# Gate products one step behind their one-hots, and the last group's v tiles loaded with its up tiles

## The chip, the cores and the metric

The kernel runs on one core of one Trainium2 chip, as one program. The metric is the device time of one execution in microseconds. Before the change three timed executions took 3132.31, 3131.12 and 3117.97 us, median 3131.12 us; a fourth execution was profiled.

## The reference, cut to what matters

The reference is one layer of an encoder over 1024 tokens of width 1024, in float32. A mixing part (a convolution module and an RWKV-7 recurrence beside each other) ends in an output projection and a layer norm. The second part is a retrieval over 128 x 128 = 16384 experts of one neuron each. The change touches the second part only:

```
q = (h2 @ peer_wq).reshape(bsz, seq, 8, 256)
s1 = einsum('bshd,hnd->bshn', q[..., :128], peer_k1)
s2 = einsum('bshd,hnd->bshn', q[..., 128:], peer_k2)
...                                   # top 16 of each, top 16 of the 256 sums
experts = i1 * 128 + i2 ;  gates = softmax(top scores)
z = einsum('td,tkd->tk', h, peer_u[experts])
y2 = einsum('tk,tkd->td', gelu(z) * gates, peer_v[experts])
x = layer_norm(ALPHA * x + gate2 * y2, ln2_g, ln2_b)
```

## The kernel before

**Two ways to the retrieval.** The 1024 tokens are eight tiles of 128. For three of them (tiles 5 to 7) the kernel gathers the rows of the chosen experts with indirect DMAs that POOL issues (L1273), and DVE sums them up (L1279, L1286). For the other five (the dense tiles, 640 tokens) it computes all 16384 experts with matmuls, and multiplies each expert's activation by a gate that is zero for experts that the token did not choose. That takes a matrix of gates with one entry for each token and expert, which has to be built first.

**The gate matrix.** `gate_matrix` is a generator, one for each dense tile, that the rest of the program steps. For each token the matrix is the product of two one-hot matrices: the first index of each of the token's 128 choices, and the second index times the gate. Eight tokens at a time, DVE compares the indices with a row of numbers (two `mask` tiles, L1094). Four tokens at a time, a quad, the masks become float32 operands: `oa` by ACT (L1100), `ob` by POOL for three tokens (L1101) and by ACT for the fourth (L1103). Then four matmuls `mgate<-oa,ob` (L1108), and ACT copies the result into a `stage` tile (L1109); after eight quads the stage is written to memory (G_d, L1116). A tile has 32 quads, so the five tiles have 160 quads and 640 product matmuls. Buffers: two for `oa`, three for `ob`, three for the masks, three PSUM banks for `mgate`, two stages.

**What steps it.** In the first stretch of the program (conv, RWKV, up to about 1000 us) `fill` calls `step(gates)` each 12th time. Then follows a loop, `while side or slow or gates`, in which the out-projection of the last tokens (L870, its norm on DVE from L874), the query projection (L216), the keys (L942, copied out by ACT at L945) and the choice of the top 16 are the side work. Each 12th turn it calls `step(gates)` inside `tc.high_priority(offset=GPRI)`, so that everything a step emits is put forward. The order of the instructions on each engine is then fixed by a scheduler with priorities, which has its own model of times; each engine runs its instructions in that order, and waits where an operand is not there. SP issues the plain DMAs, ACT those of the stages, POOL the gathers.

**The dense loop.** 32 groups follow, each of four e's (128 experts apiece). An e's up matmuls (L1418, 48 of them into two PSUM banks) are followed by a gelu on ACT (L1420), the multiplication by the gates on DVE (L1422), and a split into a high part `ah` (ACT, L1423) and a low part `al` (DVE, L1424); the down matmuls (L1434) take three products of high and low parts. The weights are split as they come: a load into a `raw` buffer (L1310, three buffers for u and v tiles), the high part by ACT (L1314), the low part by POOL (L1316: `ulo`, `vlo`). A group's v tiles are loaded two e's later than its u tiles. For group 31 each v tile is multiplied by a row of gate2 first (DVE, L1312).

**The end.** `finish` runs the down products of group 31, and ends the five dense tiles. It loads the last two v tiles, loads the five residual tiles `xres` into buffers that become free (two with the tag raw, two in uhi, one in ulo), finishes the gathers, multiplies the sums by gate2 (L1358), adds them to the residuals (L1363 on DVE, L1361 on POOL), and then for each tile and half adds the down product (L1372, for the last tile L1375), takes the norm, and multiplies and adds its two rows (ACT L1391, DVE L1392 and L1393), before the store (L1394).

## Time and profile before

| | us |
|---|---|
| median of the three timed executions | 3131.12 |
| profiled execution | 3123.78 |
| its span in the trace | 3122.0 |
| granted TensorE clock, mean | 0.968 |
| first stages, up to | 1000 |
| out-projection, queries and gate work | 1000 to 1285 |
| gate quads behind the last query matmul | 1285 to 1322.7 |
| dense loop and gathers | 1322.7 to 3102.3 |
| behind PE's last matmul | 3102.3 to 3122 |

PE is TensorE, DVE VectorE, ACT ScalarE, POOL GpSimd, and SP the engine that issues plain DMAs. A row of a stretch gives the busy time of each engine in it. A row of a group of instructions gives the line, the engine, the operation, the tiles as out<-in and the count, then the busy time and the mean of one in ns, and behind the second bar the idle time of the engine just before them and what ended it. The chain of waits is followed back from the last instruction, and its rows give a start, a length and what ran. A matmul in float32 leaves two records here, so "x8" of gate products in the chain is one quad.

### The profile page before, as it was taken

The numbers are of one execution on the slowest core, as the hardware profiler recorded it, in microseconds if no ns is written. First come the engines' busy times: TensorE is split into PE (matmuls) and PEld (weight loads), VectorE is DVE, ScalarE is ACT, GpSimd is POOL, SyncE is SP. The second block draws the span as 40 slices with busy tenths as digits, with TensorE's granted clock in tenths as the row PEclk, the third lists the DMA queues.
The fourth block names the chain that finished last, engine by engine and source line by source line (L and its number), as shares of the span: only waits on it lengthen the run. The fifth ranks groups of instructions, "written<-read, shape, count | busy, mean of one in ns | idle before, by whom it ended". The sixth has DMA issues, their size and how long they took to land.

```text
span 3122.0 us, 54848 instructions
## 1 busy us (share of the span) xinstructions
PE 2942.9 (94%) x20416; PEld 2604.9 (83%) x20416; DVE 2393.5 (77%) x5392; ACT 1186.8 (38%) x2238; POOL 1810.1 (58%) x1419
## 2 busy tenths in 40 slices
PE   6979999988899889999999999999999999999997
PEld 4748667877778788898998899989899898999986
DVE  6276764446877989369999999987888787777878
ACT  5562452333346667842322323322223232222324
POOL 2434112224253443487776786877778677787874
PEclk9989999969889999999999999999999999999998
DMA  8868766768666887899999998999999989999995
GB/s 312 312 207 301 265 183 205 268 221 299 216 217 241 314 332 278 327 350 336 328 330 327 316 344 314 352 352 330 339 344 338 356 322 340 341 338 349 328 352 196
DMA packets 431852, 945.77 MB, mean 303 GB/s; under 512 B 92465, under 2 KB 234209, under 8 KB 411105
## 3 DMA queue, kind: packets, MB, share of 16 engines
q1 hardware_dynamic: 318112, 497.62, 47.2%
q0 software_dynamic: 110592, 402.70, 34.5%
q10 hardware_dynamic: 2880, 41.94, 3.3%
q8 instruction: 160, 2.62, 0.3%
q14 instruction: 108, 0.88, 0.1%
HBM read 800.76 MB, written 141.39 MB: 302 GB/s over the span
## 4 chain that ended last, share of the span: by engine, by line
PE 64%; DVE 20%; DMA 7%; ACT 4%; issue 3%; POOL 1%; SPq 0%; ACTq 0%; DVEq 0%; POOLq 0%
PE mg L1418 23%; PE md L1434 22%; PE mm L216 7%; PE mm L870 2%; DMA cw<-cond_w 2%; DVE grow L1279 2%; PE mm L528 2%; DVE mask L1094 1%; PE mgate L1108 1%; DVE gy L1286 1%; DVE cw L303 1%; PE bank L707 1%; DMA grow<-peer_v,eid 1%; PE bank L733 1%; DVE oh L1023 1%
## 5 line engine op out<-in xcount | busy, mean ns | idle before, releaser
L1418 PE MATMUL mg<-h2h,uhi 128*128 128x320 f32 x2024 | 626.6, 310 | 7.3 <-DVE al L1424 6.5
L1418 PE MATMUL mg<-h2h,ulo 128*128 128x320 f32 x2024 | 625.9, 309 | 0.0
L1418 PE MATMUL mg<-h2l,uhi 128*128 128x320 f32 x2024 | 625.6, 309 | 0.0
L1434 PE MATMUL md<-vhi,al 128*128 128x512 f32 x1260 | 490.6, 390 | 0.0
L1434 PE MATMUL md<-vlo,ah 128*128 128x512 f32 x1260 | 489.1, 390 | 0.0
L1434 PE MATMUL md<-vhi,ah 128*128 128x512 f32 x1260 | 485.1, 390 | 1.9 <-DVE yacc L1452 1.9
L1286 DVE SCALAR_TENSOR_TENSOR gy<-grow,gz,gy 128x1024 f32<-128x1024 f32 x349 | 446.1, 1278 | 10.7 <-DMA grow<-peer_v,eid 9.6
L1279 DVE SCALAR_TENSOR_TENSOR grow<-grow,gh 128x1024 f32<-128x1024 f32 x365 | 438.1, 1210 | 16.2 <-DMA grow<-peer_u,eid 12.7
L1273 POOL DMA_INDIRECT grow<-peer_u,eid x365 | 344.5, 944 | 176.3 <-DVE grow L1279 58.0
L1273 POOL DMA_INDIRECT grow<-peer_v,eid x352 | 333.2, 947 | 164.9 <-DVE gy L1286 62.1
L1418 PEld LDWEIGHTS mg<-h2h,uhi 128*128 128x128 f32 x2024 | 380.4, 188 | 15.0 <-DVE al L1424 8.4
L1418 PEld LDWEIGHTS mg<-h2l,uhi 128*128 128x128 f32 x2024 | 380.5, 188 | 5.8
L1418 PEld LDWEIGHTS mg<-h2h,ulo 128*128 128x128 f32 x2024 | 380.4, 188 | 2.9
L1316 POOL TENSOR_TENSOR vlo<-vraw,vhi 128x1024 fp32r<-128x1024 f32 x128 | 309.1, 2416 | 26.2 <-ACT vhi L1314 22.5
L1316 POOL TENSOR_TENSOR ulo<-uraw,uhi 128x1024 fp32r<-128x1024 f32 x128 | 309.3, 2417 | 21.6 <-ACT uhi L1314 19.1
L1452 DVE TENSOR_TENSOR yacc<-md,yacc 128x512 f32<-128x512 f32 x300 | 204.6, 685 | 130.9 <-PE md L1434 97.7
L1434 PEld LDWEIGHTS md<-vlo,ah 128*128 128x128 f32 x1260 | 236.5, 188 | 47.5
L1434 PEld LDWEIGHTS md<-vhi,ah 128*128 128x128 f32 x1260 | 236.1, 188 | 47.3 <-DVE yacc L1452 2.8
L1434 PEld LDWEIGHTS md<-vhi,al 128*128 128x128 f32 x1260 | 236.5, 188 | 44.2
L1101 POOL TENSOR_TENSOR ob<-mask,selt 128x384 f32<-128x384 bf16 x160 | 140.4, 891 | 228.8 <-DVE mask L1094 99.3
L1314 ACT ACTIVATE vhi<-vraw 128x1024 fp32r<-128x1024 f32 x128 | 134.9, 1054 | 348.0 <-DMA vraw<-peer_vt 296.1
L204 POOL TENSOR_TENSOR wsplit<-wraw,wsplit 128x1024 fp32r<-128x1024 f32 x46 | 112.5, 2448 | 215.1 <-ACT wsplit L203 204.8
(430 smaller groups left out, 5868.6 us busy)
## 6 DMA issues: line engine op xcount, KB each, us to landing
uraw<-peer_ut SPq DMA_DIRECT2D x128, 512.0 KB
vraw<-peer_vt SPq DMA_DIRECT2D x128, 512.0 KB
wsplit<-split_wq SPq DMA_DIRECT2D x48, 1024.0 KB
G_d<-stage ACTq DMA_DIRECT2D x20, 2048.0 KB
gmat<-G_d SPq DMA_DIRECT2D x32, 1024.0 KB
cw<-cond_w SPq DMA_DIRECT2D x48, 512.0 KB
wsplit<-split_w_out SPq DMA_DIRECT2D x24, 1024.0 KB
split_w_in<-wsplit SPq DMA_DIRECT2D x22, 1024.0 KB
```

The lines of the kernel that those rows point to most:

```text
L204: G.tensor_sub(lo, raw, hi.bitcast(F32))
L216: T.matmul(pt, l[:, k, :], r[k], start=i == 0, stop=i == 3 * KD - 1)
L528: T.matmul(pt[:, 128 * g:128 * g + 128], dg[:, 128 * j:128 * j + 128], ubuf[ct][:, g, LAGS - 1 - m:LAGS - 1 - m + 128], start=m == 0, stop ...
L1101: G.tensor_mul(ob[:, :3], mb[:, :3], gt[:, c:c + 3, None].to_broadcast([128, 3, 128]))
L1273: G.indirect_dma_start(out=r, out_offset=None, in_=peer_u if k < 128 else peer_v, in_offset=bass.IndirectOffsetOnAxis(ap=eid[:, k % 128:k ...
L1279: V.scalar_tensor_tensor(r, r, 1.0, ht, op0=OP.mult, op1=OP.mult, accum_out=z[:, i:i + 1])
L1286: V.scalar_tensor_tensor(y, r, z[:, i - 128:i - 127], y, op0=OP.mult, op1=OP.add)
L1314: A.activation(hi, raw, AF.Copy)
L1316: G.tensor_sub(lo, raw, hi.bitcast(F32))
L1418: T.matmul(p, l[:, k, :], r[k][:, bs], start=i == 0, stop=i == 3 * KD - 1)
L1434: T.matmul(p, l[:, ts], r[:, e % 2, :], start=e == 0 and q == 0, stop=e == 3 and q == 2)
L1452: ins = V.tensor_add(ya, p, ya)
```

## The change

Three edits. **First**, the body of `gate_matrix` is cut in two: `operands` makes the masks and the one-hots of a quad, `products` its matmuls, the eviction and the store. The generator yields after each, and the products of a quad come after the operands of the next one. Both callers step twice now; in the second loop only the first of the two steps, which emits operands, stands inside `high_priority`. **Second**, each v tile of group 31 is loaded in its own e, beside the u tile, and no more in `finish`. **Third**, the residual tiles take three raw and two uhi buffers, and the small sums `fsum` move to a pool with four buffers.

```
--- before.py
+++ after.py
@@ -643,6 +643,7 @@
             slow_step(1)
         if gb and fills[0] % GSTEP == 0:
             step(gates)
+            step(gates)
 
     def pairs(n, fn):
 
@@ -1079,41 +1080,61 @@
         gt = st[:, 2]
         key = [gv[:, w].bitcast(BF).rearrange("p (t two) -> p t two", two=2) for w in range(2)]
         sh = [128, 8, 64, 2]
-        for r0 in range(0, 128, TB):
-            blocks[0] += 1
-            if st3 and tt != DT[-1] and blocks[0] % 3 == 0:
-                stage = st3[0].tile([128, 128, TB], F32, name="stage3")
+        masks = []
+
+        def operands(c):
+
+            if c % 8 == 0:
+                masks[:] = []
+                for w in range(2):
+                    m = gb[0].tile([128, 8, 128], BF, name="mask", bufs=MB)
+                    V.tensor_tensor(m.rearrange("p t (e two) -> p t e two", two=2),
+                                    iota_b.rearrange("p (e two) -> p e two", two=2)[:, None].to_broadcast(sh),
+                                    key[w][:, c:c + 8, None, :].to_broadcast(sh), op=OP.is_equal)
+                    masks.append(m)
+            ma, mb = (m[:, c % 8:c % 8 + 4] for m in masks)
+            oa, ob = quad_("oa", GB[0]), quad_("ob", GB[1])
+            A.activation(oa, ma, AF.Copy)
+            G.tensor_mul(ob[:, :3], mb[:, :3], gt[:, c:c + 3, None].to_broadcast([128, 3, 128]))
+            if c // 4 % 4 in COLA:
+                A.activation(ob[:, 3], mb[:, 3], AF.Copy, scale=gt[:, c + 3:c + 4])
             else:
-                stage = gb[0].tile([128, 128, TB], F32, name="stage", bufs=2)
-            for q in range(0, TB, 4):
-                c = r0 + q
-                if q % 8 == 0:
-                    masks = []
-                    for w in range(2):
-                        m = gb[0].tile([128, 8, 128], BF, name="mask", bufs=MB)
-                        V.tensor_tensor(m.rearrange("p t (e two) -> p t e two", two=2),
-                                        iota_b.rearrange("p (e two) -> p e two", two=2)[:, None].to_broadcast(sh),
-                                        key[w][:, c:c + 8, None, :].to_broadcast(sh), op=OP.is_equal)
-                        masks.append(m)
-                ma, mb = (m[:, q % 8:q % 8 + 4] for m in masks)
-                oa, ob = quad_("oa", GB[0]), quad_("ob", GB[1])
-                A.activation(oa, ma, AF.Copy)
-                G.tensor_mul(ob[:, :3], mb[:, :3], gt[:, c:c + 3, None].to_broadcast([128, 3, 128]))
-                if c // 4 % 4 in COLA:
-                    A.activation(ob[:, 3], mb[:, 3], AF.Copy, scale=gt[:, c + 3:c + 4])
+                V.tensor_mul(ob[:, 3], mb[:, 3], gv[:, 2, c + 3:c + 4].to_broadcast([128, 128]))
+            return oa, ob
+
+        stage = [None]
+
+        def products(c, oa, ob):
+
+            q = c % TB
+            if q == 0:
+                blocks[0] += 1
+                if st3 and tt != DT[-1] and blocks[0] % 3 == 0:
+                    stage[0] = st3[0].tile([128, 128, TB], F32, name="stage3")
                 else:
-                    V.tensor_mul(ob[:, 3], mb[:, 3], gv[:, 2, c + 3:c + 4].to_broadcast([128, 128]))
-                pt = mgate().rearrange("p (t e) -> p t e", t=4)
-                for t in range(4):
-                    T.matmul(pt[:, t, :], ob[:, t, :], oa[:, t, :], start=True, stop=True)
-                A.activation(stage[:, :, q:q + 4], pt.rearrange("p t e -> p e t"), AF.Copy)
-                yield
-            b = 4 * DT.index(tt) + r0 // TB
+                    stage[0] = gb[0].tile([128, 128, TB], F32, name="stage", bufs=2)
+            pt = mgate().rearrange("p (t e) -> p t e", t=4)
+            for t in range(4):
+                T.matmul(pt[:, t, :], ob[:, t, :], oa[:, t, :], start=True, stop=True)
+            A.activation(stage[0][:, :, q:q + 4], pt.rearrange("p t e -> p e t"), AF.Copy)
+            if q < TB - 4:
+                return
+            b = 4 * DT.index(tt) + c // TB
             part = max(i for i in range(3) if GPART[i][0] <= b)
             if part == 2:
 
-                A.activation(gfirst, stage[:, 0:4, :], AF.Copy)
-            A.dma_start(G_d[part][b - GPART[part][0]].rearrange("p g x -> p (g x)"), stage.rearrange("p e t -> p (e t)"))
+                A.activation(gfirst, stage[0][:, 0:4, :], AF.Copy)
+            A.dma_start(G_d[part][b - GPART[part][0]].rearrange("p g x -> p (g x)"), stage[0].rearrange("p e t -> p (e t)"))
+
+        made = operands(0)
+        yield
+        yield
+        for c in range(0, 128, 4):
+            now = operands(c + 4) if c < 124 else None
+            yield
+            products(c, *made)
+            made = now
+            yield
 
 
     first = inproj(1, psum, pgp)
@@ -1186,6 +1207,7 @@
         if fills[0] % TGATE == 0 or not side:
             with tc.high_priority(offset=GPRI) if GPRI else nullcontext():
                 step(gates)
+            step(gates)
 
     pg2x.close()
     dp = ctx.enter_context(tc.tile_pool(name="dp", bufs=1, side="right"))
@@ -1345,11 +1367,10 @@
         return t
 
     def finish(down, vs):
-        vs += [load_v(31, 2), load_v(31, 3)]
         xts = []
         for t in range(NT):
-            xts.append(de.tile([128, D], F32, tag="raw" if t < 2 else "uhi" if t < 4 else "ulo", name="xres",
-                               bufs=3 if t < 2 else 2))
+            xts.append(de.tile([128, D], F32, tag="raw" if t < 3 else "uhi", name="xres",
+                               bufs=3 if t < 3 else 2))
             ld(xts[t], x1_d[DT[t]])
         row_pair([(1, ln_rows[3])])
         gather_to(1)
@@ -1364,7 +1385,7 @@
         for t in range(NT):
             xt = xts[t]
             st = small.tile([128, 2, 6], F32, name="bnst")
-            sums = small.tile([128, 4], F32, name="fsum")
+            sums = gp.tile([128, 4], F32, name="fsum", bufs=4)
             for half, hs in enumerate(halves):
                 p = md() if half else mg()
                 down(t, half, p)
@@ -1406,8 +1427,8 @@
             uh, ul = u_next
             if 4 * g + e < 127:
                 u_next = load_u(4 * g + e + 1)
-            if e > 1:
-                vs.append(load_v(g, e - 2))
+            if e > 1 or g == 31:
+                vs.append(load_v(g, e if g == 31 else e - 2))
 
             ah, al = (dl.tile([128, ND], F32R, name=n_, bufs=ABUF) for n_ in ("ah", "al"))
             for bs in NBLK:
```

What each engine executes is the same in number. Up to about 1000 us, and from the last gate quad to the last group, the order is the same on every engine as well. (Lines after 646 have moved: L1108 is now L1118, L942 is L943, L1418 is L1439, L1273 L1295, L1316 L1338, L1358 L1379, L1361 L1382, L1375 and L1376 L1396 and L1397, L1392 and L1393 L1413 and L1414.)

On PE, about the last key matmuls of the query, with the first up matmul of the dense loop behind them, before:

```order
L1108 MATMUL mgate<-oa,ob 128x128 x4
L216 MATMUL mm<-h2hi,wsplit 128x256
L216 MATMUL mm<-h2lo,wsplit 128x256
L216 MATMUL mm<-h2hi,wsplit 128x256
L942 MATMUL mm<-keys,qt 128x128
L1108 MATMUL mgate<-oa,ob 128x128 x4
L942 MATMUL mm<-keys,qt 128x128 x5
L1108 MATMUL mgate<-oa,ob 128x128 x4
L942 MATMUL mm<-keys,qt 128x128 x2
L1108 MATMUL mgate<-oa,ob 128x128 x8
L1418 MATMUL md<-h2h_14171,uhi 128x320
```

and now:

```order
L1118 MATMUL mgate<-oa,ob 128x128 x4
L216 MATMUL mm<-h2lo,wsplit 128x256
L216 MATMUL mm<-h2hi,wsplit 128x256
L943 MATMUL mm<-keys,qt 128x128 x6
L1118 MATMUL mgate<-oa,ob 128x128 x8
L943 MATMUL mm<-keys,qt 128x128 x2
L1118 MATMUL mgate<-oa,ob 128x128 x8
L1439 MATMUL md<-h2h_14171,uhi 128x320
```

The keys end with fewer products ahead of them: 104 of the 640 product matmuls stood behind the last key matmul, and 136 do now. In both kernels 48 up matmuls stand among these, and the last 84 and 85 products follow without any. Farther ahead, at the last twelve matmuls of the out-projection, 16 products stood directly ahead and 12 behind; now 8 ahead and 27 behind.

On POOL, near the end, from the sums of two tiles with gate2 to the last low parts of group 31 (gland is the buffer of the very last gather), before:

```order
L1358 TENSOR_TENSOR yacc<-yacc,gmat 128x1024
L1273 DMA grow<-peer_v,eid 128x1024
L1358 TENSOR_TENSOR yacc<-yacc,gmat 128x1024
L1316 TENSOR_TENSOR vlo<-vraw,vhi 128x1024
L1273 DMA grow<-peer_v,eid 128x1024 x2
L1316 TENSOR_TENSOR ulo<-uraw,uhi 128x1024
L1273 DMA grow<-peer_v,eid 128x1024 x3
L1273 DMA gland<-peer_v,eid 128x1024
L1316 TENSOR_TENSOR ulo<-uraw,uhi 128x1024
L1316 TENSOR_TENSOR vlo<-vraw,vhi 128x1024 x2
L1361 TENSOR_TENSOR xres<-xres,yacc 128x1024
```

and now:

```order
L1379 TENSOR_TENSOR yacc<-yacc,gmat 128x1024
L1338 TENSOR_TENSOR vlo<-vraw,vhi 128x1024
L1295 DMA grow<-peer_v,eid 128x1024
L1379 TENSOR_TENSOR yacc<-yacc,gmat 128x1024
L1338 TENSOR_TENSOR vlo<-vraw,vhi 128x1024
L1295 DMA grow<-peer_v,eid 128x1024
L1338 TENSOR_TENSOR ulo<-uraw,uhi 128x1024
L1295 DMA grow<-peer_v,eid 128x1024 x4
L1338 TENSOR_TENSOR ulo<-uraw,uhi 128x1024
L1295 DMA gland<-peer_v,eid 128x1024
L1338 TENSOR_TENSOR vlo<-vraw,vhi 128x1024 x2
L1382 TENSOR_TENSOR xres<-xres,yacc 128x1024 x2
```

Between the first sum and the last gather stood one vlo and one ulo; now two vlo and two ulo stand there, and the two residual adds follow each other.

On DVE, at the end, from the last tile's second add (xres<-md) on, before:

```order
L1375 TENSOR_TENSOR xres<-md,xres 128x512
L1384 TENSOR_SCALAR bnmv<-fsum 128x1
L1376 BN_STATS bnst<-xres 128x6
L1392 TENSOR_TENSOR xres<-xres,gmat 128x512
L230 BN_AGGR bnmv<-bnst 128x2
L1392 TENSOR_TENSOR xres<-xres,gmat 128x512
L1393 TENSOR_TENSOR xres<-xres,gmat 128x512
L1392 TENSOR_TENSOR xres<-xres,gmat 128x512
L1393 TENSOR_TENSOR xres<-xres,gmat 128x512
L1392 TENSOR_TENSOR xres<-xres,gmat 128x512 x2
L1393 TENSOR_TENSOR xres<-xres,gmat 128x512
L1392 TENSOR_TENSOR xres<-xres,gmat 128x512
```

and now, up to the same add, which is the last row:

```order
L1413 TENSOR_TENSOR xres<-xres,gmat 128x512
L1414 TENSOR_TENSOR xres<-xres,gmat 128x512
L1413 TENSOR_TENSOR xres<-xres,gmat 128x512
L238 RECIPROCAL rstd<-rstd 128x1
L240 TENSOR_SCALAR bnmv<-bnmv 128x1
L1396 TENSOR_TENSOR xres<-mg,xres 128x512
L1414 TENSOR_TENSOR xres<-xres,gmat 128x512
L1405 TENSOR_SCALAR bnmv<-fsum 128x1
L1414 TENSOR_TENSOR xres<-xres,gmat 128x512
L239 TENSOR_TENSOR rnew<-rstd 128x1
L1397 BN_STATS bnst<-xres 128x6
L1396 TENSOR_TENSOR xres<-md,xres 128x512
```

Before, all 20 multiplications and additions with the norm's rows stood behind that add. Now eight stand ahead of it, five of them in these rows, and twelve behind. The multiplications of the v tiles (before L1312) stood behind one another over the last group's rows; the first two now stand among the sums ahead of them.

## The prediction

> **What bounds the kernel now.** I read the page's share of busy time first, then the same by stage, then the groups of instructions of the stages that the change touches, then single rows there.
>
> ```profile
> PE 2942.9 (94%) x20416; PEld 2604.9 (83%) x20416; DVE 2393.5 (77%) x5392; ACT 1186.8 (38%) x2238; POOL 1810.1 (58%) x1419
> ```
> ```profile
> 1000.00:1120.00 120.00, 94.15 (x657) 84.16 (x653) 105.39 (x425) 77.91 (x176) 47.55 (x49) 0.96 0.84 307
> 1120.00:1285.00 165.00, 153.91 (x1291) 149.70 (x1289) 135.26 (x522) 122.59 (x282) 72.86 (x78) 1.00 0.83 314
> 1285.00:1322.70 37.70, 33.82 (x246) 30.80 (x247) 13.71 (x21) 35.15 (x78) 20.13 (x23) 1.00 0.74 263
> 1322.70:3102.30 1779.60, 1770.39 (x9932) 1614.23 (x9930) 1507.63 (x2655) 514.96 (x855) 1353.01 (x1028) 1.00 0.93 334
> 3102.30:3122.00 19.70, 0.00 (x0) 0.00 (x0) 15.51 (x45) 8.87 (x16) 0.00 (x0) 0.55 0.36 133
> ```
>
> The columns of the second fence are the stretch, its length, the busy time of PE, weight loads, DVE, ACT and POOL, then the granted clock, the DMA share and GB/s. PE bounds the whole, and most of it is the dense loop, 1322.70 to 3102.30, where PE is busy 1770.39 of 1779.60 us. The program order there is the same before and after, so that stretch gets nothing. What is left for the change is small: the two stretches in which gate work runs beside the out-projection and the queries (1000 to 1285), the gate tail behind the last query matmul (1285 to 1322.7), where ACT is busy 35.15 of 37.70 us and so sets the pace, and the end behind PE's last matmul, where only DVE and ACT work.
>
> ```profile
> L1108 PE MATMUL mgate<-oa,ob 128*128 128x128 f32 x880 | 117.2, 280 | 24.9 <-POOL ob L1101 13.2 <-ACT oa L1100 9.7 <-ACT stage L1109 1.7
> L1094 DVE TENSOR_TENSOR mask<-iota_b,selbank 128x1024 bf16<-128x1024 bf16 x107 | 71.3, 673 | 30.2 <-ACT oa L1100 13.1 <-ACT ob L1103 9.0 <-ACT selt L1074 5.8
> ```
>
> Both rows are for 1000 to 1285. PE stood 24.9 us in front of gate products: 13.2 for POOL's half of the one-hots, 9.7 for ACT's, 1.7 for an eviction. This is all that a later product can save. The masks themselves stood 30.2 us, nearly all behind ACT.
>
> **Gate stretch, step 1: products leave the query.** By the order, 104 product matmuls (26 quads of four tokens) stood behind the last key matmul of the query; now 136 (34 quads) do. So 8 quads go from the query, where PE paces, to the tail, where ACT paces.
>
> ```profile
> 1242.84 0.89 PE mgate L1108 x8
> ```
>
> A row of the chain counts two records to a matmul, so x8 is one quad: 0.89 us. The query ends 8 x 0.89 = **7.1 us earlier**.
>
> **Step 2: the tail gets longer.** Its steady pace is read from two evictions four quads apart, and what one quad costs ACT there from the groups:
>
> ```profile
> 1303.56 0.61 ACT L1109 ACTIVATE stage<-mgate 128x512 f32<-128x512 f32 x1
> ...
> 1308.71 0.64 ACT L1109 ACTIVATE stage<-mgate 128x512 f32<-128x512 f32 x1
> ```
> ```profile
> L1109 ACT ACTIVATE stage<-mgate 128x512 f32<-128x512 f32 x26 | 16.0, 626 | 0.3 <-PE mgate L1108 0.3
> L1100 ACT ACTIVATE oa<-mask 128x512 f32<-128x512 bf16 x24 | 15.8, 660 | 2.2 <-PE mgate L1108 2.2
> L1103 ACT ACTIVATE ob<-mask,selt 128x128 f32<-128x128 bf16 x23 | 8.7, 434 | 0.0
> ```
>
> (1308.71 - 1303.56) / 4 = 1.29 us for a quad, and ACT hardly waits. The order puts 34 evictions and 32 of each ACT one-hot behind ACT's last key copy, before 26, 24 and 23. Eight more quads cost 8 x 1.29 = **10.3 us**. The 48 dense matmuls that the order lets into this tail are 48 in both kernels, so they cover no more of it than before.
>
> **Step 3: waits of PE in the query.** A product stands one step behind its one-hots, so the short ACT operation directly ahead of it should be done: I take the waits on ACT as recovered, 9.7 + 1.7 = **11.4 us**. I leave the 13.2 on POOL's half, since POOL follows the masks, DVE is busy (105.39 + 135.26) of 285 us there, 84%, and the same masks and selections remain. Bounds: 0, if the waits only move, and 24.9, if all go. The front (out-projection, last tiles) is inside this term: its last 12 matmuls have x8 products directly ahead instead of x16, and x27 directly behind.
>
> The gate stretch gives -7.1 + 10.3 - 11.4 = -8.2 us, from -21.7 to +3.2 by the bounds. What SP and DVE get is covered: DVE has 36 mask operations between the last front tile and the last transpose before, 27 now, the others stand ahead; the last four h2t loads move behind score writes on SP, but seven quads of the tail still stand ahead of their first use.
>
> One rule bears on step 3.
>
> ```profile
> 1090.00:1100.00 10.00, 7.80 (x62) 7.38 (x60) 10.00 (x43) 5.25 (x13) 4.41 (x5) 1.00 0.98 399
> 1100.00:1110.00 10.00, 9.69 (x55) 9.00 (x56) 1.86 (x10) 2.41 (x5) 1.03 (x2) 0.83 0.94 358
> ...
> 1100.31 0.95 PE L1108 MATMUL mgate<-oa,ob 128*128 128x128 f32 x4 [2.50 <-POOL ob L1101]
> ```
>
> Behind a wait of 2.50 us the granted clock was 0.83 for ten us; a wait of this kind that goes would save up to 10 x 0.17 = 1.7 us beside itself. The Trainium skill, "TensorE: Matmul & The Clock Gate", Part 1 (The HAM clock gate), says that the clock is halved only after an idle window of about 3.4 us; by that rule a wait of 2.50 us costs no clock and the term is 0. The trace shows a loss all the same, and I leave the 1.7 out of the sum because this wait is one on POOL, which I keep.
>
> **The dense loop: 0.** Its rows stand in the same order on every engine.
>
> **The end, step 4: DVE's queue behind the last matmul.**
>
> ```profile
> 3101.90 0.39 PE L1434 MATMUL md<-vlo,ah 128*128 128x512 f32 x1
> ```
> ```profile
> 3116.74 0.69 DVE L1392 TENSOR_TENSOR xres<-xres,gmat 128x512 f32<-128x512 f32 x1
> 3117.35 1.29 DVE L1393 TENSOR_TENSOR xres<-xres,gmat 128x512 f32<-128x512 f32 x2
> ```
> ```profile
> L1392 DVE TENSOR_TENSOR xres<-xres,gmat 128x512 f32<-128x512 f32 x10 | 6.7, 683 | 0.8 <-ACT xres L1391 0.8
> L1393 DVE TENSOR_TENSOR xres<-xres,gmat 128x512 f32<-128x512 f32 x10 | 6.6, 684 | 0.0
> ```
>
> All 20 half-row operations of the last norm ran behind PE's last matmul. In the changed order tiles 0 and 1 are complete earlier, and 8 of the 20 stand ahead of the last tile's add. They start 0.60 us apart (3116.74 to 3117.35), so 8 x 0.60 = **4.8 us** go from the end. The first two tiles' adds come earlier too, but PE's 120 last matmuls are the same, so that alone moves nothing.
>
> **Step 5: POOL's queue ahead of the last gather.** This is the price of having the v tiles early.
>
> ```profile
> 3058.06 2.42 POOL L1316 TENSOR_TENSOR ulo<-uraw,uhi 128x1024 fp32r<-128x1024 f32 x1
> ...
> 3064.37 0.94 POOL L1273 DMA_INDIRECT gland<-peer_v,eid  x1 [0.31 <-issue]
> 3065.33 2.43 POOL L1316 TENSOR_TENSOR ulo<-uraw,uhi 128x1024 fp32r<-128x1024 f32 x1
> 3067.70 4.77 POOL L1316 TENSOR_TENSOR vlo<-vraw,vhi 128x1024 fp32r<-128x1024 f32 x2
> ```
> ```profile
> 3064.37 11.24 DMA gland<-peer_v,eid
> ...
> 3078.44 0.16 DVE al L1424
> ```
>
> The last gather (gland) was issued at 3064.37 and landed 11.24 us later; DVE waited for it, and the last al, which PE's last down products need as soon as the up matmuls end, stands behind it in DVE's queue. In the changed order one more vlo and the last ulo stand ahead of this gather: 2 x 2.42 = 4.84 us of POOL, which had no gap over 0.31 us there. So gland lands near 3080.4, al is ready 4.8 us later, and PE waits for it: **+4.8 us**. Bounds: 0, if POOL's queue has room or the gather lands faster, and about +6, if the add of a first tile (1.21 us, below) that now stands ahead of the gather's sum comes on top. The end is then -4.8 + 4.8 = 0, from -4.8 to +1.2.
>
> ```profile
> 3078.84 1.21 DVE L1363 SCALAR_TENSOR_TENSOR xres<-xres,yacc 128x1024 f32<-128x1024 f32 x1
> ...
> 3083.73 3.31 DVE L1363 SCALAR_TENSOR_TENSOR xres<-xres,yacc 128x1024 f32<-128x1024 f32 x1
> ```
> ```profile
> 3083.55 2.41 POOL L1316 TENSOR_TENSOR vlo<-vraw,vhi 128x1024 fp32r<-128x1024 f32 x1 [0.48 <-ACT vhi L1314]
> ```
>
> The same add took 1.21 us alone and 3.31 us beside a vlo of 2.41 us. The Trainium skill, "SBUF — State Buffer" (Who interferes with whom), says that a DVE operation with two SBUF inputs and a GpSimd operation that reads SBUF exclude each other through a shared port pair; the trace agrees here, with 2.1 us. This speaks against the change: POOL's two xres adds now stand together, amid DVE's adds of this form. By the rule up to two more meetings would cost 4.2 us of DVE; by the rows PE goes on with its down products until 3101.90, 18 us behind the slow add, so it is hidden, and the sum gets 0.
>
> **Sum.** -7.1 + 10.3 - 11.4 - 4.8 + 4.8 = -8.2 us. The profiled execution took 3123.78 us (span 3122.0), so its like would take 3115.6. It stands between the timed runs (3117.97, 3131.12, 3132.31); the middle two of all four have a mean of 3127.45, and 3127.45 - 8.2 = 3119.
>
> **Rivals.** (1) The step of distance covers all waits, POOL's too: 13.2 us more, -21.4, so 3127.45 - 21.4 = 3106. For it: masks are put forward alone, and they had waited 22.1 us behind ACT's one-hots, which no longer stand behind evictions put forward with them. Against: DVE at 84% and only three mask buffers. (2) The change doesn't do what it says: the scheduler had already put products where they were ready, the waits only move to other quads, and the query's gain is given back in the tail: -7.1 + 10.3 = +3.2, so 3131. For it: PE waits for gate products only 24.9 of 285 us. (3) Slower: the one-hots and not ACT's copies pace the tail. A stretch where eight quads took long is
>
> ```profile
> 1240.02 1.16 PE mgate L1108 x8
> ...
> 1256.46 0.91 PE mgate L1108 x8
> ```
>
> (the first and the last of eight quads in the chain: (1256.46 - 1240.02) / 7 = 2.35 us a quad). If masks and POOL's half can deliver a quad only each 2.35 us, also when no query work is left, 34 quads take 79.9 us where 26 took 26 x 1.29 = 33.5: +46.4, and no wait is recovered: -7.1 + 46.4 = +39.3, so 3167. It decides as soon as the one-hots come slower than ACT's 1.29 us. Against: the tail's DVE was busy 13.71 and POOL 20.13 of 37.70 us.
>
> **How the numbers follow.** Forecast 0.50 (3112 to 3126), rival 1 0.20, rival 2 0.22, rival 3 0.08. Range 3104 to 3136: it takes in most of rival 1 (less the end's gain on top) and rival 2 with the end's upper bound, and leaves out rival 3. About 0.5% (15.7 us) is what a measurement of this kernel can tell from no change: faster is under 3115.5, which is rival 1 and a quarter of the forecast, 0.33; slower is over 3146.8, rival 3, 0.08; the rest is 0.59.
>
> **What would show it.** Step 1: the last key matmul ends 7 us (with step 3, 18) earlier. Step 2: the first dense stretch begins 10 us later behind it, evictions 1.29 us apart. Step 3: idle time before the gate products near 13 us, on POOL alone. Step 4: 12 half-row operations behind PE's last matmul, and 11 us from it to the end instead of 16. Step 5: gland issued near 3069 on the old scale and a gap of 4 to 5 us of PE before its last ten down groups. It is wrong if the order's quads in the tail run apart from ACT's pace, if PE has no gap at the end, or if the dense loop changes its length.

## The result: 19 us slower, and the profile after

| | before | after |
|---|---|---|
| median of 15 timed runs, us | 3122.64 (3116.38 to 3133.92) | 3141.93 (3126.26 to 3158.54) |
| profiled execution, us | 3123.78 | 3143.16 |
| its span, us | 3122.0 | 3141.4 |

The ratio is 1.0056 with a 95% interval of 1.0045 to 1.0066: the change makes the kernel slower by 0.56%; the two medians lie 19.3 us (0.62%) apart. Forecast were 3119 and a range of 3104 to 3136.

First the line of busy time on the page of after, to be set beside the one of before:

```profile
PE 2959.7 (94%) x20416; PEld 2618.8 (83%) x20416; DVE 2381.6 (76%) x5392; ACT 1188.7 (38%) x2238; POOL 1810.7 (58%) x1419
```

The work is the same in number, and the mean granted clock is 0.961, where it was 0.968. The windows of after show where, cut at its own landmarks (columns as in the prediction: the stretch, its length, busy PE, weight loads, DVE, ACT, POOL, then granted clock, DMA share, GB/s):

```profile
1000.00:1120.50 120.50, 95.42 (x653) 86.66 (x653) 98.12 (x406) 74.32 (x169) 46.26 (x48) 0.89 0.80 292
1120.50:1280.50 160.00, 149.44 (x1232) 144.86 (x1232) 129.85 (x530) 113.53 (x257) 65.68 (x69) 0.99 0.79 296
1280.50:1337.50 57.00, 45.77 (x324) 41.48 (x322) 21.59 (x32) 48.40 (x107) 28.32 (x33) 0.94 0.77 285
1337.50:3121.60 1784.10, 1773.41 (x9939) 1613.95 (x9937) 1503.80 (x2653) 517.04 (x856) 1352.97 (x1028) 1.00 0.93 333
3121.60:3141.40 19.80, 0.00 (x0) 0.00 (x0) 16.10 (x46) 7.67 (x15) 0.00 (x0) 0.62 0.36 132
```

The third row is the gate tail: 57 us, with the clock at 0.94, where before had 1.00. ACT, which was to set its pace, is busy 85% of it, where it was 93% in the tail of before: something else holds it up.

For a comparison by stage each trace was cut at the start of the last matmul of each kind: out-projection (L870, now L871), keys (L942, L943), gate products (L1108, L1118), up (L1418, L1439) and down (L1434, L1455). The front runs from the first gate product to the last matmul of the out-projection, the query from there to the last key matmul, the tail to the last gate product, the end from the last down matmul to the end of the span. "Before again" is a second profile of the unchanged kernel.

| us | front | query | tail | dense | down | end |
|---|---|---|---|---|---|---|
| before | 213.8 | 170.6 | 39.1 | 1753.9 | 26.2 | 20.1 |
| before again | 221.1 | 171.6 | 39.1 | 1753.2 | 26.7 | 20.5 |
| after | 226.1 | 160.0 | 57.0 | 1757.8 | 25.9 | 20.2 |
| after minus before | +12.3 | -10.6 | +17.9 | +3.9 | -0.3 | +0.1 |

With -3.9 us ahead of the first product these make the 19.4 us of the two spans. The tail is the one stage that is longer by far. The front of the first profile was itself a short one: the same program took 221.1 in another execution. The granted clock tells the two apart. These are 20 us, 40 us behind the first gate product, first in before and then in before again:

```profile
938.30:958.30 20.00, 18.05 (x253) 16.19 (x250) 15.20 (x40) 12.76 (x29) 10.29 (x10) 1.00 0.54 207
```
```profile
934.60:954.60 20.00, 18.05 (x169) 15.94 (x166) 12.40 (x35) 9.67 (x22) 8.45 (x8) 0.57 0.40 162
```

PE is busy 18.05 us in both, but at a clock of 0.57 it gets 169 matmul records done and not 253. After has 0.66 in the same place. So about 7 of the front's 12.3 us are no sign of the change, and about 5 stay, which go with a load that met a store (below). The dense stage, whose order is the same, ran between 1749.8 and 1757.8 us over all profiles, which is how well a single profile tells it.

### The query is shorter, but less of it by waits

Waits of PE on gate products inside the query (what PE waited for, us in total, times, longest), before from 1112 to 1283:

```profile
PE mgate L1108 <- ACT oa L1100: 7.9, 10, 1.4
PE mgate L1108 <- POOL ob L1101: 5.2, 4, 3.2
```

and after from 1121 to 1281:

```profile
PE mgate L1118 <- POOL ob L1098: 4.3, 4, 1.7
PE mgate L1118 <- ACT oa L1097: 2.5, 3, 2.2
```

The eight quads gone are 7.1 us; the waits on ACT fell by 5.4 and on POOL by 0.9. Other small waits came in, and the clock was 0.99 where it was 1.00. Together the query lost 10.6.

### The tail waits for loads

The waits of SP's queue in after, between 1255 and 1345, and PE's waits from 1275 on:

```profile
SPq L1218 <- DMA G_d<-stage: 13.8, 1, 13.8
SPq L1218 <- DMA h2h<-h2t_d: 2.7, 3, 1.3
```
```profile
PE md L1439 <- DMA h2h<-h2t_d: 4.7, 3, 4.0
PE mgate L1118 <- ACT oa L1097: 4.4, 17, 1.8
```

L1218 loads the 16 tiles of h2 (h2h and h2l) that the dense matmuls multiply. SP stood 13.8 us in front of the first of them until a store of a gate stage had landed; in before this row does not exist. In the code, the pool of these tiles is opened right after the pools with the third stage and the front's pages are closed (`pg2x.close()`), so they take that memory. The store is the 15th of the 20, the last one that the third stage holds; in before it had gone out at 1253.47, 15.7 us earlier. The issues show it, the store on ACT's queue and the first load on SP's in after:

```profile
1269.18 0.33 ACTq L1127 DMA_DIRECT2D G_d<-stage  x1
```
```profile
1277.46 0.32 SPq L1218 DMA_DIRECT2D h2h<-h2t_d  x1
```

and the same load in before:

```profile
1261.51 0.44 SPq L1196 DMA_DIRECT2D h2h<-h2t_d  x1
```

How long such a store takes from issue to landing is on the page of one experiment (e3) that has a time for it, 7.6 us as the last number of the row:

```profile
G_d<-stage ACTq DMA_DIRECT2D x20, 2048.0 KB, 7.6
```

1269.18 + 7.6 = 1276.8 is within a microsecond of the load's issue. So the loads start 16 us later by the clock and 18 us later against the last key matmul, which comes 2.2 us earlier. Late loads then meet the next 2 MB store (issued at 1287.15), as after's chain of waits shows:

```profile
1280.20 6.05 DMA h2h<-h2t_d
1286.27 12.32 DMA h2h<-h2t_d
1298.63 0.90 PE md L1439 x2
```

Dense matmuls stand among the products in PE's order, so a dense matmul that waits for its load holds up the products behind it, and with them ACT's evictions.

### The front waits for a load beside a store

Three views of after: a wait of PE in the front that before doesn't have, the load in the chain of waits, and the windows of 15 us there, where the clock is the third number from the end:

```profile
PE mm L871 <- ACT hf L260: 10.3, 1, 10.3
```
```profile
1012.99 2.31 DMA rwkv_d<-yo
1015.36 7.89 DMA ycf<-conv_d
```
```profile
1015.00:1020.00 5.00, 0.17 (x2) 0.00 (x0) 4.88 (x21) 0.94 (x3) 0.00 (x0) 0.70 0.89 349
1020.00:1025.00 5.00, 0.00 (x0) 0.00 (x0) 0.02 (x1) 1.65 (x4) 0.92 (x2) 0.50 0.91 243
1025.00:1030.00 5.00, 4.50 (x17) 4.15 (x18) 3.72 (x13) 3.62 (x10) 3.13 (x4) 0.50 0.88 283
```

The load of ycf, 128 KB, was on its way with a gate store that ACT had issued 0.14 us behind it, at 1015.50:

```profile
1015.50 0.34 ACTq L1127 DMA_DIRECT2D G_d<-stage  x1
```

In before the store went out 2.22 us behind the load, when it had nearly landed:

```profile
1015.04 3.01 DMA ycf<-conv_d
```
```profile
1017.26 0.33 ACTq L1116 DMA_DIRECT2D G_d<-stage  x1
```

7.89 us against 3.01. The Trainium skill, "DMA: Bandwidth & Descriptors", section "Queues, rings and completion order", says that a DMA engine takes turns, packet by packet, between the queues that have work for it; by that rule a small load beside a large store on another queue gets a part of each engine until it is through, which fits the two rows. The clock was 0.50 from 1020 to 1030, in the second half of PE's standing and in the first five us of work behind it.

Other profiles repeat it: the store went out 0.11 us behind the load in e3 and 0.01 in e8, the load took 7.70 and 7.56 us, and PE waited 10.1 and 12.0. In e1 and e9, whose gate work is the same, the store went out 0.66 us behind the first such load, which landed in 2.9 us, and PE has no such wait. So a fraction of a microsecond between two queues, and not the order alone, decides whether the front pays.

### The end: DVE, not PE, is late

The last gather (POOL), and on DVE the last tile's last add, after:

```profile
3087.30 0.95 POOL L1295 DMA_INDIRECT gland<-peer_v,eid  x1 [0.16 <-DVE gy L1308]
```
```profile
3116.15 2.28 DVE L239 TENSOR_TENSOR rnew<-rstd 128x1 f32<-128x1 f32 x2
...
3127.62 0.67 DVE L1396 TENSOR_TENSOR xres<-md,xres 128x512 f32<-128x512 f32 x1
```

and the same add before:

```profile
3102.93 0.69 DVE L1375 TENSOR_TENSOR xres<-md,xres 128x512 f32<-128x512 f32 x1
```

PE's last matmul started at 3121.18 in after:

```profile
3121.18 0.39 PE L1455 MATMUL md<-vlo,ah 128*128 128x512 f32 x1
```

So the last add stands 6.4 us behind PE's last matmul, where it stood 1.0 us behind (3102.93 against 3101.90). The eight row operations did move ahead of it, as the order says; they now run while the add waits its turn. From the add to the end of the span it is 13.8 us, before 19.1: the 5 us that left the stretch behind the add stand ahead of it.

### The profile page after: what moved, and what is told of

Its sections match the earlier page's. It is cut to its first block, busy times and chain, and to the rows that moved or that the text cites. A ratio compares the mean times of both kernels' runs of the same rounds, so it can differ in the third digit from the quotient of the medians.

```text
span 3141.4 us, 54905 instructions
## 1 busy us (share of the span) xinstructions
PE 2959.7 (94%) x20416; PEld 2618.8 (83%) x20416; DVE 2381.6 (76%) x5392; ACT 1188.7 (38%) x2238; POOL 1810.7 (58%) x1419
## 4 chain that ended last, share of the span: by engine, by line
PE 64%; DVE 16%; DMA 6%; issue 3%; ACT 2%; POOL 1%; SPq 0%; DVEq 0%; ACTq 0%; POOLq 0%
PE mg L1439 23%; PE md L1455 21%; PE mm L216 6%; PE mm L871 3%; PE mgate L1118 2%; DVE grow L1301 2%; PE mm L528 2%; DMA cw<-cond_w 1%; DVE gy L1308 1%; DVE yacc L1473 1%; DVE mask L1091 1%; PE bank L708 1%; PE bank L734 1%; PE bank L676 1%; DMA vraw<-peer_vt 1%
## 5 line engine op out<-in xcount | busy, mean ns | idle before, releaser
L1439 PE MATMUL mg<-h2h,uhi 128*128 128x320 f32 x2024 | 626.1, 309 | 9.3 <-DVE al L1445 9.3
L1439 PE MATMUL mg<-h2h,ulo 128*128 128x320 f32 x2024 | 625.0, 309 | 1.0 <-POOL ulo L1338 1.0
L1439 PE MATMUL mg<-h2l,uhi 128*128 128x320 f32 x2024 | 625.4, 309 | 0.0
L1455 PE MATMUL md<-vhi,al 128*128 128x512 f32 x1260 | 491.2, 390 | 0.0
L1455 PE MATMUL md<-vlo,ah 128*128 128x512 f32 x1260 | 490.3, 391 | 0.0
L1455 PE MATMUL md<-vhi,ah 128*128 128x512 f32 x1260 | 486.3, 391 | 0.4 <-DVE yacc L1473 0.4
L1295 POOL DMA_INDIRECT grow<-peer_u,eid x365 | 345.0, 945 | 174.6 <-DVE grow L1301 59.1
L1295 POOL DMA_INDIRECT grow<-peer_v,eid x352 | 333.6, 948 | 162.2 <-DVE gy L1308 64.2
L1439 PEld LDWEIGHTS mg<-h2h,uhi 128*128 128x128 f32 x2024 | 379.9, 188 | 17.9 <-DVE al L1445 12.7
L1439 PEld LDWEIGHTS mg<-h2l,uhi 128*128 128x128 f32 x2024 | 379.9, 188 | 5.6
L1439 PEld LDWEIGHTS mg<-h2h,ulo 128*128 128x128 f32 x2024 | 379.9, 188 | 4.2 <-POOL ulo L1338 1.3
L1338 POOL TENSOR_TENSOR vlo<-vraw,vhi 128x1024 fp32r<-128x1024 f32 x128 | 308.8, 2413 | 33.4 <-ACT vhi L1336 28.1
L1338 POOL TENSOR_TENSOR ulo<-uraw,uhi 128x1024 fp32r<-128x1024 f32 x128 | 309.2, 2415 | 21.0 <-ACT uhi L1336 18.1
L1455 PEld LDWEIGHTS md<-vlo,ah 128*128 128x128 f32 x1260 | 236.5, 188 | 48.8
L1455 PEld LDWEIGHTS md<-vhi,ah 128*128 128x128 f32 x1260 | 236.1, 188 | 45.9 <-DVE yacc L1473 0.6
L1455 PEld LDWEIGHTS md<-vhi,al 128*128 128x128 f32 x1260 | 236.5, 188 | 45.1
L216 PE MATMUL mm<-hhi,wsplit 128*128 128x512 f32 x672 | 226.9, 411 | 10.2 <-ACT gsig L399 5.4
```

The costliest lines, as they stand in the source:

```text
L216: T.matmul(pt, l[:, k, :], r[k], start=i == 0, stop=i == 3 * KD - 1)
L1295: G.indirect_dma_start(out=r, out_offset=None, in_=peer_u if k < 128 else peer_v, in_offset=bass.IndirectOffsetOnAxis(ap=eid[:, k % 128:k ...
L1338: G.tensor_sub(lo, raw, hi.bitcast(F32))
L1439: T.matmul(p, l[:, k, :], r[k][:, bs], start=i == 0, stop=i == 3 * KD - 1)
L1455: T.matmul(p, l[:, ts], r[:, e % 2, :], start=e == 0 and q == 0, stop=e == 3 and q == 2)
```

## The experiments

All but e5 are timed in rounds against the kernel before on the same chip, and each ratio has its 95% interval. The kernel before had medians of 3124.29 us beside e1 to e4, 3124.64 beside e6 to e8, 3121.89 beside e9 to e12.

**e1, the gate's part alone.** The gate work as in after, the end as in before.

```
-            if e > 1 or g == 31:
-                vs.append(load_v(g, e if g == 31 else e - 2))
+            if e > 1:
+                vs.append(load_v(g, e - 2))
...
+        vs += [load_v(31, 2), load_v(31, 3)]
```

> The split of gate_matrix and its steps alone, with the v tiles, residual tiles and small sums of the last group as before. Theory 1 (all of the loss is made by the gate work: the first up matmuls wait for the h2h tiles, and a tail of 34 quads): about +15 us on the kernel before, near 3138, with the last gate product some 16 us later than before and the h2h loads issued near 1277 instead of 1261. Theory 2 (the loss is mostly in the last group): near 3126, within 4 us of the kernel before.

Measured: ratio 1.0037 (1.0023 to 1.0052), median 3137.25. In its profile the query took 159.6 us and the tail 57.2, as in after, and the same two waits stand there:

```profile
SPq L1218 <- DMA G_d<-stage: 14.0, 1, 14.0
```
```profile
PE md L1440 <- DMA h2h<-h2t_d: 5.1, 2, 4.8
```

So the gate's part alone loses, and query and tail together lose 6 to 7 us (216.8 against 209.7 and 210.7). This profiled execution, 3126.23 us, was the fastest of its eleven, so it shows the stages and not the whole median.

**e2, the end's part alone.** Gate as before; v tiles, residual buffers and fsum as in after.

```
-            if e > 1:
-                vs.append(load_v(g, e - 2))
+            if e > 1 or g == 31:
+                vs.append(load_v(g, e if g == 31 else e - 2))
```

> The v tiles of the last group loaded with its up tiles, the residual tiles and small sums moved, and the gate work as before. Theory 1: the two terms of the end cancel, so between -2 and +4 us of the kernel before; its last up matmuls wait 1 to 2 us for POOL's low parts, and the stretch behind PE's last matmul is as long as before (20 us). Theory 2: +15 us. The prediction's own step 4 alone, without step 5, would give -5.

Measured: 1.0027 (1.0013 to 1.0041), median 3133.39. The end loses too, by 4 to 13 us, where -2 to +4 were expected. Its POOL and DVE rows:

```profile
3075.41 0.95 POOL L1273 DMA_INDIRECT gland<-peer_v,eid  x1 [0.16 <-issue]
```
```profile
3087.15 2.14 DVE L1362 SCALAR_TENSOR_TENSOR xres<-xres,yacc 128x1024 f32<-128x1024 f32 x1 [3.00 <-DMA grow<-ln_rows]
...
3108.34 2.22 DVE L1391 TENSOR_TENSOR xres<-xres,gmat 128x512 f32<-128x512 f32 x1
```

The residual add waits 3.00 us for a row that is loaded late, with al and the gather's sum behind it in DVE's queue (after doesn't have this wait), and two operations take over 2 us beside POOL's (2.39 us from 3085.82, 2.37 from 3107.64). PE waited in this stretch for one ulo alone, 1.0 us. From the last sum of group 30 to the end of the span the five profiles with early v tiles took 76.1 us in the mean (74.2 to 78.0), the nine without them 73.8 (72.6 to 74.7): 2.3 us.

**e7, the buffers alone.** Only the residual tags and the fsum pool of after.

```
-            xts.append(de.tile([128, D], F32, tag="raw" if t < 2 else "uhi" if t < 4 else "ulo", name="xres",
-                               bufs=3 if t < 2 else 2))
+            xts.append(de.tile([128, D], F32, tag="raw" if t < 3 else "uhi", name="xres",
+                               bufs=3 if t < 3 else 2))
```

> The kernel before with the new buffers of the residual tiles and of the small sums alone; the v tiles come late as before. Theory 1 (the early v tiles push the last gather back by 4.9 us on POOL, and DVE's chain to the end with it): the last gather is issued 15.8 us behind the last sum of group 30 as before (20.6 with the early v tiles), the rest from that sum to the end is 73 us or less, and the time within 3 us of the kernel before. Rival (the residual tiles' new buffers cost): 76 us there and +5.

Measured: 1.0004 (0.9991 to 1.0017), median 3126.79: no effect. The last gather was issued 15.8 us behind the sum, as expected, and from the sum to the end it took 74.2 us, where 73 or less were expected. What e2 loses beyond this comes with the early v tiles.

**e3, the third stage free earlier.** After, but the third stage isn't used for the last two dense tiles, so its memory is free before the loads of h2.

```
-                if st3 and tt != DT[-1] and blocks[0] % 3 == 0:
+                if st3 and tt not in DT[-2:] and blocks[0] % 3 == 0:
```

> The changed kernel, with one more condition: the fourth dense tile doesn't use the third stage buffer, whose memory the h2h tiles take afterwards. Theory 1a (the late evictions hold that memory, the h2h loads wait for them, and PE's first up matmuls for the loads): the h2h loads are issued near 1262 again, PE's wait of 4.7 us for them goes, and the time is 5 to 10 us under the changed kernel, 3132 to 3137. Theory 1b (the tail is long only because 34 quads stand behind the query at ACT's pace): no change, 3142 within 3.

Measured: 1.0059 (1.0036 to 1.0081), median 3145.2. The time missed the expected 3132 to 3137. The mechanism showed: the first load was issued at 1251.53, PE never waited for h2h, the clock in the tail was 1.00, and the tail took 49.1 us for 32.5 quads.

```profile
1251.53 1.97 SPq L1218 DMA_DIRECT2D h2h<-h2t_d  x1
```
```profile
1285.10:1334.20 49.10, 42.70 (x310) 38.15 (x309) 19.04 (x29) 45.57 (x101) 26.88 (x32) 1.00 0.63 237
```

But PE waited 9.1 us on ACT in the query, once for 6.6, and the query was 170.4 again:

```profile
PE mgate L1118 <- ACT oa L1097: 9.1, 4, 6.6
```

That one-hot was late because ACT itself stood: ahead of a gate store, which it issues, until a load of h2h had landed.

```profile
1271.78 0.33 ACTq L1127 DMA_DIRECT2D G_d<-stage  x1
1272.15 0.63 ACT L1097 ACTIVATE oa<-mask 128x512 f32<-128x512 bf16 x1 [8.90 <-DMA h2h<-h2t_d]
```

So what the tail gained by early loads the query gave back, to a good part by the same loads.

**e4, the products put forward too.** After with both steps inside `high_priority`.

```
             with tc.high_priority(offset=GPRI) if GPRI else nullcontext():
                 step(gates)
-            step(gates)
+                step(gates)
```

> The changed kernel with products and evictions put forward as well, as their one-hots are: the second step stands inside the priority too. By the order 25 quads stand behind the last key matmul (34 in the changed kernel, 26 before). Theory 1 (the products that are no longer put forward make the loss): the last gate product and the dense loop come 12 to 18 us earlier than in the changed kernel, 3124 to 3130. Rival (the step of lag makes the loss, whatever is put forward): 3140 or more.

Measured: 1.0081 (1.0062 to 1.0101), median 3151.78, the slowest of all, where 3124 to 3130 were expected. Query 170.0 and tail 39.2 us are those of before, with 25 quads in the tail: it is the lost priority of the products that carries quads into the tail, not the distance of one step. But the front took 227.3 us and the end 23.6. In the front PE's waits on ACT's one-hots are 7.0 us,

```profile
PE mgate L1118 <- ACT oa L1097: 7.0, 7, 2.8
```

where both profiles of before have 1.8:

```profile
PE mgate L1108 <- ACT oa L1100: 1.8, 4, 0.8
```

**e5, before again.** The kernel before, unchanged.

> The kernel before once more, for a second profile of it. Theory 1 (the query and the tail together make the loss in the gate stretch): from the last out-projection matmul to the last gate product again 209 to 211 us (217 in both profiles with the split gate work). If the stretch ahead of it (first gate product to the last out-projection matmul), 213.8 us in the first profile and 221.0 in the run with the end alone, both with the same order, differs again by some us, then the 221 to 227 of the changed kernels there is no sign of the change.

Measured in one profiled run: 3128.59 us, front 221.1 and not 213.8, the stages behind it within 1 us. The front has two lengths without any change of order, and the first profile had the short one (the clock, above).

**e6, e10 and e11, no lag.** After with a quad's products emitted in the same pair of steps as its own operands: e6 with after's end, e10 with the end of before, e11 as e10 with the third stage in another turn (`blocks[0] % 3 == 1`, see e9).

```
-        made = operands(0)
-        yield
-        yield
         for c in range(0, 128, 4):
-            now = operands(c + 4) if c < 124 else None
+            made = operands(c)
             yield
             products(c, *made)
-            made = now
             yield
```

> The changed kernel without the lag: products come in the same pair of steps as their own one-hots, but are still not put forward. Theory 1 (products not put forward lengthen the tail; 32 quads stand behind the last key matmul by the order, 34 in the changed kernel): the tail is 52 to 56 us, and the time within 6 us of the changed kernel, 3136 to 3148. Rival (the lag of a step makes the loss): 3128 or less.

> The gate work split but without the lag, products not put forward, and the end as before. Theory 1 (the early v tiles cost 4 to 9 us by themselves, and without the lag the gate stretch is as long as before: 429 us from the program's first product's offset to the last one against 431): 4 to 9 us under the 3137 of the same with the early v tiles, 3128 to 3133, and from the last sum of group 30 to the end 73 to 74 us (78.0 with the early v tiles). Rival (the end costs nothing): 3137.

> As the run without the lag and with the end as before, and with the third stage used two blocks earlier. Theory 1: PE's wait for h2h (2.9 us without the lag) goes, the tail is 3 to 5 us shorter (48 to 50), and the time is at or a little under the kernel before, 3118 to 3126. Rival: no change against the run without the lag.

Measured: e6 1.0038 (1.0026 to 1.0051), e10 1.0050 (1.0029 to 1.0072), e11 1.0054 (1.0035 to 1.0073). Query 155.4 to 157.8, tail 52.5 to 53.0 us with 32 quads in it. The distance of one step is not what costs: without it query and tail are much the same, and the kernel as slow. Two expectations were missed. e10 was to be 4 to 9 us faster than e6, since it lacks the early v tiles; by the medians e6 is 12.7 us above the kernel before and e10 12.5, so here the rival (the end costs nothing) holds. e11 was to have loads that come early; its edit does the opposite, as e9 shows.

**e8, more steps.** The gate part alone, stepped each 10th turn, so that fewer quads are left for the tail.

```
-TGATE = 12
+TGATE = 10
```

> The split gate work alone (the end as before), stepped each 10th turn instead of each 12th, so that 22 quads instead of 34 stand behind the last key matmul. Theory 1 (each quad costs 0.89 us beside the query and 1.5 in the tail): the query gets 11 us longer than with each 12th turn, the tail about 20 us shorter, and the time is 7 to 12 us under the 3137 of the split alone. Rival (ACT or DVE is the bound over the query as well): the query gets longer by as much as the tail gets shorter, 3137 within 4.

Measured: 1.0027 (1.0008 to 1.0046), median 3136.23. Tail 35.0 us with 22 quads, query 176.6: of the 22.2 us that left the tail against e1, 17.0 came back in the query, more than the 11 expected. The query's clock was 0.96, in e1 0.99, so a part of it is slower matmuls. The expected 7 to 12 us of gain didn't come.

**e9, the third stage in another turn.** The gate part alone, `blocks[0] % 3 == 1`, so that the third stage is released at another time. The expectation counts blocks 1, 4, 7, 10 and 13, but the condition takes block 16 too (16 % 3 is 1, and it is the last block of the fourth dense tile). So the memory comes free one block later than in after, and not two earlier.

> The split gate work alone (the end as before), with the third stage buffer used for blocks 1, 4, 7, 10 and 13 instead of 3, 6, 9, 12 and 15, so that its memory, which the h2h tiles take, comes free two blocks (16 quads) earlier. The number of stages and of quads behind the last key matmul (34) stays. Theory 1 (the late products hold that memory, and the tail waits for the h2h loads): the wait of PE for h2h, 5.1 us with the split alone, goes, the tail is 50 to 52 us instead of 57, the query stays at 160, and the median is 4 to 8 us under the 3137 of the split alone. Rival (the tail is 34 quads at ACT's pace): tail 57, time unchanged.

Measured: 1.0036 (1.0014 to 1.0058), median 3132.74. The first load went out at 1277.62, 10 us behind the last key matmul. Until 1270.6 two writes of scores stood ahead of it in SP's order and waited for ACT, then a load of u waited 6.4 us for POOL, and the store of block 16 landed at 1277.54:

```profile
SPq L948 <- ACT s L946: 18.9, 1, 18.9
```
```profile
1271.21 6.33 DMA G_d<-stage
```

The tail took 55.8 us. By name PE waited only 0.2 us for h2h; 1.98 us ahead of the first dense matmul, for which the view names no releaser, ended as that load landed, and the waits on gate products were 9.1 us (6.1 in after). Since the memory came free later, this run doesn't test what an early release is worth; e3 does.

**e12, the turn of before.** The kernel before with `blocks[0] % 3 == 2`.

> The kernel before with the third stage used for blocks 2, 5, 8, 11 and 14, one block earlier; the scheduler then leaves 21 quads behind the last key matmul instead of 26. Theory 1 (quads behind the query cost 1.5 us, beside it 0.89 us unless ACT binds there, as more steps showed): tail 32 us instead of 39, query 4 to 8 us longer, time within 4 of the kernel before. Rival (a shorter tail is worth its quads): 5 us or more under it.

Measured: 1.0025 (1.0010 to 1.0041), median 3130.95. Query 182.0, tail 33.8 us with 21 quads; the loads went out at 1250.3, since 14 is the last block in the third stage. The time is 9.1 us above the kernel before by the medians, where 4 at most were expected. The query took 11.4 us more for five quads, which at 0.89 us are 4.5; its clock was 0.96, in before 1.00, and an estimate from that, 182 x 0.04 = 7 us, covers the rest. Whether early loads alone would gain in before stays open.

No kernel of these beat the one before.

## Why the prediction was wrong, step by step

**Where it started.** It set 3127.45 us for before, from four runs; the median of fifteen is 3122.64. From its own change of -8.2 to the measured +19.3 there are 27.5 us.

**Step 1, eight quads leave the query (-7.1): right.** 34 quads stand in the tail, and PE's matmul records in the query fell from 1298 to 1232, by 66, where eight quads are 64. Both profiles of the split gate have a query of 160 us (after, e1) against 171.

**Step 2, the tail gets longer (+10.3): the pace nearly right, the tail wrong by 7.6.** Five profiles whose first load of h2h went out 21 us or more ahead of the last key matmul, and in which PE waits no more than 0.2 us for h2h, give the price of a quad: 33.8 us for 21 quads (e12), 35.0 for 22, 39.2 for 25, 39.1 for 26 (before), 49.1 for 32.5 (e3). Over the whole that is (49.1 - 33.8) / 11.5 = 1.33 us, from before to e3 10.0 / 6.5 = 1.54. Eight quads are then 10.6 to 12.3 us, and the tail would have been 50 to 51 us long. It was 57. The six profiles whose loads went out 5.4 us ahead of the last key matmul at most, or behind it, all lie 4 to 6 us above that line: 52.5 to 53.0 for 32 quads, 55.8 to 57.2 for 34. **One of the two steps that failed is the sentence in step 3 that the last h2t loads "move behind score writes on SP, but seven quads of the tail still stand ahead of their first use", costed at nothing.** Not the last four but all sixteen came late, 18 us against the last key, held by one store at the head of SP's queue. The tail paid 4.7 us of PE's waits for it (5.1 in e1), and about 1 us more is left (57.0 - 51 - 4.7), beside a clock of 0.94. I had counted what stood ahead of the loads in the order, but not whose memory they take. e3 shows the cover back: no wait, clock 1.00, 49.1 us. e9 shows that score writes and a load of u can hold the loads as long.

**Step 3, waits on ACT recovered (-11.4): the other step that failed, with a third of it gained.** The query's waits on ACT fell by 5.4 us, but beyond the eight quads it became only 3.5 us shorter: 7.9 us less than the sum had. In the front no gain shows: e1's front is 221.3 us, as before's longer one, and after's is 226 with a new wait of 10.3 us for ycf, a collision of load and store that the order doesn't show. e4 speaks against the thought that a step of distance cures these waits by itself: with it, and both steps put forward, PE waited 7.0 us on ACT's one-hots in the front and 6.3 in the query, and before 9.7 in both.

**The price of moving a quad** was in the prediction's numbers (7.1 against 10.3 us for eight): 0.89 us in the query, against 1.33 to 1.54 measured in the tail. Eight of them cost 3.5 to 5.2 us net, and that can only be paid for by waits. Waits gave 3.5 to 4 (10.6 - 7.1 in after), late loads took 5 to 6. That is the 6 to 7 us which query and tail lose in e1.

**Rival 3, slower, had the right sign and the wrong cause.** One-hots didn't pace the tail; by e3's tail 34 quads without the loads' wait take 49.1 + 1.5 x 1.33 = 51 us, and not 80. Rival 2 came nearest in kind, what the query gains the tail gives back, at +3.2 us; e8 and e3 show that exchange from both sides.

**Step 4, eight row operations ahead of the last add (-4.8): the move was right, the gain nil.** It took DVE's queue as waiting for PE. It stood 1.0 us behind PE before and 6.4 now: the same operations ahead of the add only push it back. Behind the last matmul 20.2 us remain, before 20.1. The sign that the prediction gave, 11 us instead of 16, was off from the start: its own row has 19.70 us for this stretch, and 15.51 is DVE's busy time in it.

**Step 5, the last gather later (+4.8): the delay right, its path wrong.** From the last sum of group 30 gland was issued 20.7 us later, before 15.8: +4.9, and the last al started 6.2 us behind the start of the last up matmul, before 2.7. But PE waited 0.3 us at most for an al, since other down products stood ahead; a gap of PE was the sign that the prediction had set. DVE paid instead. The runs that tell the end's cost disagree: the profiles with early v tiles are 2.3 us longer from the last sum of group 30, e2's median is 6.6 us above e7's and after's 6.3 further above the kernel before than e1's, but e6 and e10, which differ by the end alone, stand at +12.7 and +12.5. So a cost of 2 us shows in the profiles, and how much the end costs in the median stays open.

**The sum.** Against the prediction's -8.2, the profile of after has 7.9 us less gain in the query (10.6 for the 18.5 of steps 1 and 3), 7.6 more in the tail, 12.3 more in the front, 3.9 more in the dense loop and 3.9 less ahead of the first product: with the last two columns of the table 27.6, the whole distance. Of the front's 12.3, 7 belong to the short front of before's first profile; against before again the spans differ by 14.6 us, of which the tail has 17.9 and the query -11.6. The rounds share it out so: e1 +13.0 us and e2 +9.1 by their medians make 22, and both together 19.3.

Two things stay open. The front takes 214 or 221 us with the same order, and the clock goes with it, 1.00 or 0.57 over 20 us; why it was lower in one execution than in another no run shows. And e1's median lies 11 us above its own profile, whose query and tail explain 6 to 7 of the 13 us that it loses; the granted clock was 0.962 in the median of its runs and 0.964 in that profile.

## What to carry to other kernels

Work that moves behind the stage it ran beside costs the difference between its prices in the two places, and a wait can only pay for it as far as a profile shows that wait; put both prices in one line before counting the gain. When an order moves, look not only at what stands ahead of each load but at whose memory the load takes and when that is released, since one load at the head of a queue that waits for a store holds all behind it. On the path's last microseconds ask which engine really finishes last: moving its own operations to ahead of its own last operation gains nothing. And check what an experiment's edit does against the trace: `% 3 == 1` took one block more than was counted, and turned the test round.

## What the runs showed of the hardware

A store of 2 MB issued 0.14 us behind a load of 128 KB stretched it from 3.01 to 7.89 us, on another queue; issued 2.22 us behind, it did not. e1 has both in one pair of loads: the store 0.66 us behind the first and 0.08 behind the second, which landed in 2.91 and 7.64 us. With the same order and the same matmuls the granted clock was 1.00 over 20 us in one profile and 0.57 in another, which made 7 us of the front. Two operations of DVE on 128 x 1 elements took 2.28 us at 3116.15 (the row in the part on the end), on the chain of the end, where POOL had this running:

```profile
3115.95 2.40 POOL L1258 TENSOR_TENSOR grow<-grow 128x1024 f32<-128x1024 f32 x1 [7.71 <-DVE bnmv L240]
```

The Trainium skill, "SBUF — State Buffer", section "SBUF: two separate sides", has the shared port pair as a lock that is held for the whole instruction, not a bandwidth that is split; the trace agrees: even an operation on 128 numbers waits as long as POOL's goes on. The same pair takes 0.22 us in before:

```profile
3111.96 0.22 DVE L239 TENSOR_TENSOR rnew<-rstd 128x1 f32<-128x1 f32 x2
```
